# The last attention head of a two-layer diffusion backbone: output products moved into its first two steps, and half a tile ahead in the others

## The chip, the cores and the metric

The kernel runs on one core of one Trainium2 chip. The metric is the device time of one execution in microseconds (us). In the profile PE is the matrix engine (PEld its weight loads), DVE the vector engine, ACT the scalar engine, POOL the GpSimd engine and SP the engine that issues most DMAs.

## The reference

Two layers over 1024 latent tokens of width 1024, with a context of 256 tokens. Layer 0 is a latent attention with 16 heads, layer 1 a differential attention with 8 heads. The change concerns the end of layer 1, where the context gets no output (`need_ctx` is false). Per head of 128 columns, with scale 1/8:

```python
def combine(o1, o2, gate):
    o = o1 - lam_full.astype(o1.dtype) * o2
    o = rms_norm(o, g_sub) * (1.0 - lambda_init)
    return gated(o, gate)                      # o * silu(gate)
q, k, v, gate = project(h, True)
q_c, k_c, v_c, gate_c = project(h_c, False)
o1, o1_c = prefix_attention(q[..0:1], k[..0], v, ...)   # softmax over 1024 + 256 keys
o2, o2_c = prefix_attention(q[..1:2], k[..1], v, ...)
...
x = layer_norm(DEEPNORM_ALPHA * x + gate[:, None, :] * (o @ out_w[i]), ln_g[i], ln_b[i])
```

`o` is 1024 x 1024 (8 heads of 128 columns), `out_w[1]` is 1024 x 1024; the output is `x` after layer 1.

## The kernel before, in words

**Tiles.** The 1024 tokens are 8 tiles `t` of 128. Layer 1 works head by head; a head takes its tiles one after the other, pipelined over three steps: scores of tile t (`scores1`, L1342 and L1343, then maxima on DVE, L1355 to L1361, exponentials on ACT, L1365, sums and the combination of the two softmaxes into one `p` on DVE, L1368 to L1371), turning `p` on PE by transposes (`turn1`, L1378, then `split16`: a half `ph` on ACT, L181, and its rest `pl` on DVE, L182), and the values (`values1`, L1386 to L1388: ten chunks of three matmuls; scaling on ACT, L1391 and L1392, rstd on POOL, L159 and L160). `step1` writes one such step: scores of tile s, values of tile s - 2, turning of tile s - 1, and between them work of a side generator.

**The last head.** In head 7 the side work is the output projection. Its input for a tile is `ws`, 128 x 1024: seven heads come from memory (`out_load`: DMA of the heads' outputs and of the gates, a product on POOL, L1479), column block 7 comes from the head itself (L1397 on DVE). `out_turn` transposes blocks of `ws` on PE (L1491) and splits them into `wx` (ACT, L176) and `wy` (DVE, L177). `mm3` (L185 to L187) is one product: three matmuls of 512 columns, hi x hi, hi x lo, lo x hi, for one block k of 8 and one half `hh` of the output. A tile has 16 products, in two PSUM banks `y[0]`, `y[1]`. `out_tile1(t)` writes them: k = 0 to 6 of half 0, k = 0 to 3 of half 1, then the turn of column block 7, k = 4 to 6 of half 1, then k = 7 of both. Then residual (L1526), layer norm (L1527 to L1543) on DVE, POOL and ACT, and the store; the last tile's layer norm has a form of its own.

**Steps.** Call step s the one with the scores of tile s; steps 8 and 9 have no scores. `out_tile1(s - 2)` runs in steps 2 to 9, `out_turns(s - 1)`, the first seven blocks of the next tile, is woven into it after its 9th and 12th yields. Tile 0's is put ahead in step 2. Steps 0 and 1 have no products. `SLOT1` and `SLOTO` are budgets in units of columns that say how much side work goes between the parts of a step.

**Order.** PE's order is the order in which the program is written (`MAN1`); the other engines' orders and DMA issues come from a scheduler, within the rotating buffers: 8 PSUM banks (tag "b"), and SBUF buffers by tag. Each engine's order is fixed when the kernel is built. The gates of head 7 go through memory like those of the others (`sg_d`); its Silu (L1327) and the split of its values into `vh`, `vl` are written by `prod_v1` in head 6's last steps and run in step 0. `out_open` splits the four late blocks (k = 4 to 7) of the output weight (`oHL`, L1468, L1469 and L176, L177); the first four (`NOW`) are there before.

## Time and profile before

| | |
|---|---|
| median of 3 runs | 1781.78 us (1780.85 to 1781.8) |
| profiled execution | 1781.43 us, span 1779.5 us (1.93 us lie around it) |
| mean granted clock | 0.992 |
| PE, DVE, ACT, POOL busy | 94%, 69%, 63%, 45% of the span |
| step 0, 1, 2 (windows) | 11.4, 9.6, 19.1 us |
| steps 3 to 7 | 17.0 us each |
| steps 8, 9 | 14.8, 13.0 us |
| after PE's last matmul | 8.5 us |

The profile gives busy time of engines in windows, instructions in order of time with the idle time before them and what ended it, and totals of waits. Times of the timeline are in us from the span's start; head 7's first score stands at 1618.34 and PE's last matmul ends at 1771.01.

### The profile page before, as it was taken

Reading aid. Unit: us, or ns where it says so; the run is one execution under the profiler, and the core shown is the slowest. Engines: PE = TensorE matmul, PEld = TensorE weight load, DVE = VectorE, ACT = ScalarE, POOL = GpSimd, SP = SyncE. Lnnn points to the kernel's source line nnn. Section 1 sums busy time; section 2 is a strip of 40 time slices with the busy share of each in tenths; the row PEclk is TensorE's granted clock in tenths of the full one; section 3 lists DMA queues with packets and bytes.
Section 4 is the critical chain, followed back from the end, with each engine's and each line's share of the span. In section 5 each row is a group of like instructions: output and inputs, shape, how many; then the busy total and the mean of one; then the engine's idle time right before and its main releaser. Section 6 shows DMA issues by size and latency. Waiting matters only on the chain. (4 is left out here: it accounts for less than half of the span.)

```text
span 1779.5 us, 36756 instructions
## 1 busy us (share of the span) xinstructions
PE 1664.8 (94%) x14564; PEld 1233.5 (69%) x14564; DVE 1230.8 (69%) x2045; ACT 1119.5 (63%) x2235; POOL 800.3 (45%) x724
## 2 busy tenths in 40 slices
PE   7999999899999998999999999999998999888998
PEld 7999966566666665577866766667675757566876
DVE  7658575665665657557747787787777777868664
ACT  2551177777777787845536676767676766758542
POOL 1532147667776676845541222222313131455454
PEclk9999999999999999999999999999999999999999
DMA  8258520111111113164432212131312122232331
GB/s 301 86 151 261 161 68 22 40 46 27 36 45 34 46 42 85 47 217 166 148 108 76 55 50 74 55 79 55 81 55 60 38 61 61 68 119 67 108 110 71
DMA packets 111225, 154.84 MB, mean 87 GB/s; under 512 B 13415, under 2 KB 84679, under 8 KB 111054
## 3 DMA queue, kind: packets, MB, share of 16 engines
q1 hardware_dynamic: 102654, 144.90, 27.1%
q10 hardware_dynamic: 8400, 7.61, 1.3%
q8 instruction: 114, 1.87, 0.5%
q14 instruction: 57, 0.47, 0.1%
HBM read 98.65 MB, written 27.07 MB: 71 GB/s over the span
## 5 line engine op out<-in xcount | busy, mean ns | idle before, releaser
L779 POOL TENSOR_TENSOR pl<-p,ph 128x1024 f16<-128x1024 f32 (+1 forms) x176 | 364.7, 2078 | 146.4 <-ACT ph L778 120.6
L1365 ACT ACTIVATE p<-ps_b,mx 128x512 f32<-128x512 f32 (+1 forms) x384 | 230.7, 618 | 84.0 <-DVE mx L1361 82.9
L777 ACT ACTIVATE p<-ps_a,esc 128x1024 f32<-128x1024 f32 (+1 forms) x176 | 189.2, 1075 | 93.2 <-PE ps_a L835 87.2
L759 DVE TENSOR_REDUCE mx<-ps_a 128x1 f32<-128x1024 f32 x128 | 155.3, 1222 | 126.9 <-PE ps_a L757 126.8
L778 ACT CAST ph<-p 128x1024 f16<-128x1024 f32 (+1 forms) x176 | 177.1, 1006 | 5.5
L1359 DVE TENSOR_REDUCE mx<-ps_b 128x1 f32<-128x512 f32 x256 | 166.0, 681 | 0.3 <-PE ps_b L1343 0.3
L848 PE MATMUL ps_d<-Vh,pl 128*128 128x65 f16 x1344 | 146.0, 194 | 3.3 <-POOL pl L779 3.3
L845 PE MATMUL ps_d<-Vh,ph 128*128 128x65 f16 x1344 | 148.1, 195 | 0.0
L847 PE MATMUL ps_d<-Vl,ph 128*128 128x64 f16 x1344 | 146.9, 193 | 0.0
L845 PEld LDWEIGHTS <-ph 128*128 128x128 f16 x1344 | 123.2, 97 | 18.0 <-issue 4.6
L1342 PE MATMUL ps_b<-KS,QS 128*128 128x512 f16 (+1 forms) x384 | 127.7, 349 | 7.5 <-DVE pl L182 4.1
L1390 POOL TENSOR_TENSOR sm<-sm,us 128x1 f32<-128x1 f32 x64 | 19.3, 302 | 252.7 <-DVE sm L1369 248.3
L847 PEld LDWEIGHTS <-ph 128*128 128x128 f16 x1344 | 123.9, 98 | 12.1
L1378 PE MATMUL ps_b<-idr,p 128*128 128x128 f32 x640 | 104.1, 278 | 29.9 <-ACT p L1365 15.7
L1343 PE MATMUL ps_b<-KS,Q 128*128 128x512 f16 (+1 forms) x384 | 130.5, 349 | 0.0
L833 PE MATMUL ps_a<-qH,KH 100*128 100x512 f16 x320 | 121.5, 380 | 9.0 <-ACT p L777 4.7
L182 DVE SCALAR_TENSOR_TENSOR pl<-ps_b,lcf,ph 128x512 f16<-128x512 f32 (+1 forms) x192 | 117.2, 654 | 13.7 <-ACT ph L181 13.6
L848 PEld LDWEIGHTS <-pl 128*128 128x128 f16 x1344 | 123.1, 97 | 4.6 <-POOL pl L779 4.6
L181 ACT ACTIVATE ph<-ps_b,lcf 128x512 f16<-128x512 f32 (+1 forms) x192 | 115.4, 649 | 17.3 <-PE ps_b L1378 17.3
L834 PE MATMUL ps_a<-qH,KL 96*128 96x512 f16 x320 | 121.3, 379 | 0.0
L835 PE MATMUL ps_a<-qL,KH 96*128 96x512 f16 x320 | 120.7, 377 | 0.0
L1378 PEld LDWEIGHTS ps_b<-idr,p 128*128 128x128 f32 x640 | 77.6, 143 | 57.1 <-ACT p L1365 24.5
(435 smaller groups left out, 5282.2 us busy)
## 6 DMA issues: line engine op xcount, KB each, us to landing
ws<-in_dw SPq DMA_DIRECT2D x28, 512.0 KB, 4.0
adw<-in_ada_w SPq DMA_DIRECT2D x24, 512.0 KB, 4.6
adaw<-in_ada_w SPq DMA_DIRECT2D x16, 512.0 KB, 7.5
g<-sg_d SPq DMA_DIRECT2D x16, 512.0 KB, 9.0
sg_d<-gg ACTq DMA_DIRECT2D x40, 128.0 KB, 3.5
o_d<-op SPq DMA_DIRECT2D x7, 640.0 KB, 3.9
xt<-in_xT SPq DMA_DIRECT2D x16, 256.0 KB, 4.6
wgs<-in_w_in SPq DMA_DIRECT2D x32, 128.0 KB, 2.3
```

What stands on the lines that cost most here:

```text
L759: dve.tensor_reduce(mx[:, t, 0:1], ps, axis=AX.X, op=ALU.max)
L777: act.activation(p32[:, :n], st, AF.Exp, scale=esc0)
L778: act.copy(ph[:, :n], p32[:, :n])
L779: pool.tensor_tensor(pl[:, :n], p32[:, :n], ph[:, :n], op=ALU.subtract)
L845: pe.matmul(pv[:, t, :], ph[:, ts], Vh[:, k, h, :], start=(k == kcs[0] and t == 0), stop=False, skip_group_check=True)
L847: pe.matmul(pv[:, t, :V0], ph[:, ts], Vl[:, k, h, :], start=False, stop=False, skip_group_check=True)
L848: pe.matmul(pv[:, t, :], pl[:, ts], Vh[:, k, h, :], start=False, stop=(k == NT - 1), skip_group_check=True)
L1342: pe.matmul(out, qs[m][:, ts], ks[m][:, c0:c0 + n], start=True, stop=False)
L1343: pe.matmul(out, q1[m][:, ts], ks[m][:, c0:c0 + n], start=False, stop=True)
L1359: dve.tensor_reduce(mx[:, 2 + 2 * m + i:3 + 2 * m + i], b, axis=AX.X, op=ALU.max, negate=True)
L1365: act.activation(p[m][:, c0:c0 + n], b, AF.Exp, bias=nb, accum_out=sm[:, 2 + 3 * m + i:3 + 3 * m + i])
L1378: pe.transpose(st[:, j * P:(j + 1) * P], pc[:, (k0 + j) * P:(k0 + j + 1) * P], idn)
```

## The change

Products of the output are spread anew over head 7's steps, in a new generator `out_step(s)`, with a tile in work `a = s - 2` and a tile ahead `b = s - 1`:

- step 0: eight products of tile 0 (both halves, k = 0 to 3), with the split of the late weights woven in; step 1: six (k = 4 to 6), with the turn of tile 1;
- step 2: seven products of tile 1, half 0, the column block of tile 0, and closing k = 7 of tile 0: nine;
- steps 3 to 7: half 1 of tile a (k = 0 to 6), with tile b's turn woven in (after 3 and 5 products), then k = 0 to 3 of half 0 of tile b, the turn of column block 7 of tile a, k = 4 to 6 of half 0 of tile b, and the closing products: sixteen;
- step 8: half 1 of tile 6, four products of tile 7, column block, closing: thirteen; step 9: the rest, twelve.

So eleven products stand between the values of a step and the column's turn. Loads of tiles 0 and 1 and tile 0's turn go into head 6's last steps. Head 7's gates stay in the chip's memory (`g7`); their Silu and the value split are written after step 1 (`out_gates`). Source lines move by one to 38 rows: L159 and L160 are now L160 and L161, L176 and L177 are L177 and L178, L182 is L183, L185 to L187 are L186 to L188, L1361 is L1369, L1365 is L1373, L1368 to L1371 are L1376 to L1379, L1397 is L1403, L1491 is L1507, L1542 and L1543 are L1580 and L1581.

```diff
+SLOTF = 0, 4800, 3200, 3200, 3200
...
-        later.append(top)
+        if h < H1 - 1:
+            later.append(top)
+        else:
+            og.update(Vf=Vf, gg=gg, uv=uv)
...
-            oo, g = og[t]
-            c = slice(h * P, (h + 1) * P)
-            dve.scalar_tensor_tensor(oo[:, c], o, ss[:, 1:2], g[:, c], op0=ALU.mult, op1=ALU.mult)
+            dve.scalar_tensor_tensor(og[t][:, DH:], o, ss[:, 1:2], og["g7"][:, t, :], op0=ALU.mult, op1=ALU.mult)
...
+    def out_gates():
+
+        vt[H1 - 1] = vh, vl = w1("vh"), w1("vl")
+        split16(vh, vl, og["Vf"], kc1)
+        prv.close()
+        wg1 = a1.enter_context(spool("a1outg", side="right"))
+        og["g7"] = wg1.tile(GG[0], GG[1], name="g7")
+        flat = lambda x: x.rearrange("p t d -> p (t d)")
+        act.activation(flat(og["g7"]), flat(og["gg"]), AF.Silu, scale=og["uv"])
...
+    def out_step(s):
+
+        a, b = s - 2, s - 1
+        early, late_ = range(NOW), range(NOW, KT - 1)
+        if s == 0:
+            yield from weave(chain(out_mm(0, 0, early), out_mm(0, 1, early)), out_split(), (0, 2, 4, 6))
+            return
+        if s == 1:
+            yield from weave(chain(out_mm(0, 0, late_), out_mm(0, 1, late_)), out_turns(1), (1, 4))
+            return
+        res = w1("res")
+        sp.dma_start(res, zn_d[a * P:(a + 1) * P, :])
+        end = SEQ // P - 1
+        if a == end:
+            yield from out_mm(a, 0, late_)
+        if a:
+            yield from weave(out_mm(a, 1, range(KT - 1)), out_turns(b), (3, 5))
+        if b <= end:
+            yield from out_mm(b, 0, early if a else range(KT - 1))
+        out_turn(a, KT - 1, 1)
+        yield 256
+        if a and b < end:
+            yield from out_mm(b, 0, late_)
+        yield from out_close(a, res)
...
-        for hh in range(2):
-            for k in range(KT - 1):
-                mm(hh, k)
-                yield 1600
-                if hh == 1 and k == 3:
-                    out_turn(t, KT - 1, 1)
-                    yield 256
...
-                    G = weave(out_tile1(t - 2), out_turns(t - 1), (9, 12)) if t >= 2 else iter(())
-                    if t == 2:
-                        G = chain(out_turns(0), G)
+                    G = out_step(t)
                     credit[0] = 0
-                step1((h, t), G, SLOT1 if not last else SLOTO)
+                step1((h, t), G, SLOT1 if not last else SLOTF if t < 2 else SLOTO)
                 if last:
                     for _ in G:
                         pass
+                    if t == 1:
+                        out_gates()
```

PE in step 4, before: the fourth product of the older tile's second half (bank ps_b_22683), the turn of the next tile's `ws_22411` between. All products of this step read `wx_22540` and `wy_22541`, which were turned in step 3:

```order
L1491 MATMUL ps_b_22732<-idr,ws_22411 128x128 x4
L185 MATMUL ps_b_22683<-oH_12515,wx_22540 128x512
L186 MATMUL ps_b_22683<-oL_12516,wx_22540 128x512
L187 MATMUL ps_b_22683<-oH_12515,wy_22541 128x512
L1491 MATMUL ps_b_22742<-idr,ws_22206 128x128
```

PE in step 4, after: the turn of tile 3's `ws_22435`, the last product of tile 2's second half (bank ps_b_22706), and the first product of tile 3 (bank ps_b_22752):

```order
L1507 MATMUL ps_b_22743<-idr,ws_22435 128x128 x3
L186 MATMUL ps_b_22706<-o_3360_22003,wx_22529 128x512
L187 MATMUL ps_b_22706<-o_3361_22004,wx_22529 128x512
L188 MATMUL ps_b_22706<-o_3360_22003,wy_22530 128x512
L186 MATMUL ps_b_22752<-oH_12509,wx_22719 128x512
L187 MATMUL ps_b_22752<-oL_12510,wx_22719 128x512
L188 MATMUL ps_b_22752<-oH_12509,wy_22720 128x512
```

The last three rows read `wx_22719` and `wy_22720`, which come from the turn in the same step.

DVE in step 4, before: the column's gate, the softmax sums and the combination, `pl`, and then `wy_22731` of tile 3:

```order
L1397 SCALAR_TENSOR_TENSOR ws_22206<-o_3472_22671,ss_22673,g_22207 128x128
L1368 TENSOR_REDUCE sm_22607<-sm_22607 128x2
L1369 RECIPROCAL sm_22607<-sm_22607 128x2
L1370 SCALAR_TENSOR_TENSOR sm_22607<-sm_22607,nlam 128x1
L1371 SCALAR_TENSOR_TENSOR p_3464_22608<-p_3465_22609,sm_22607,p_3464_22608 128x1280
L182 SCALAR_TENSOR_TENSOR pl_22700<-ps_b_22701,lcf,ph_22699 128x512
L182 SCALAR_TENSOR_TENSOR pl_22700<-ps_b_22720,lcf,ph_22699 128x512
L177 TENSOR_TENSOR wy_22731<-ps_b_22732,wx_22730 128x512
```

DVE in step 4, after: the same start, then `wy_22720` of tile 3.

```order
L1403 SCALAR_TENSOR_TENSOR ws_22282<-o_3475_22695,ss_22697,g_22280 128x128
L1376 TENSOR_REDUCE sm_22631<-sm_22631 128x2
L1377 RECIPROCAL sm_22631<-sm_22631 128x2
L1378 SCALAR_TENSOR_TENSOR sm_22631<-sm_22631,nlam 128x1
L178 TENSOR_TENSOR wy_22720<-ps_b_22721,wx_22719 128x512
L183 SCALAR_TENSOR_TENSOR pl_22732<-ps_b_22733,lcf,ph_22731 128x512
L178 TENSOR_TENSOR wy_22720<-ps_b_22743,wx_22719 128x384
L1379 SCALAR_TENSOR_TENSOR p_3467_22632<-p_3468_22633,sm_22631,p_3467_22632 128x1280
```

`wy` stands ahead of the combination now, and still behind the column's gate.

POOL in step 9, before: statistics of tile 6's layer norm (mv), the rstd (ss) of tile 7's column, then the two passes over tile 6's z:

```order
L160 TENSOR_TENSOR mv_23499<-mv_23499,neghalf 128x1
L1540 TENSOR_SCALAR mv_23499<-mv_23499 128x1
L159 TENSOR_SCALAR ss_23541<-ss_23541 128x1
L160 TENSOR_TENSOR ss_23541<-ss_23541,neghalf 128x1
L1542 TENSOR_TENSOR z_23487<-z_23487,wsq_21984 128x1024
L1543 TENSOR_TENSOR z_23487<-z_23487,gb_3254_21283 128x1024
```

POOL in step 9, after:

```order
L161 TENSOR_TENSOR mv_23514<-mv_23514,neghalf 128x1
L1578 TENSOR_SCALAR mv_23514<-mv_23514 128x1
L1580 TENSOR_TENSOR z_23497<-z_23497,wsq_22001 128x1024
L160 TENSOR_SCALAR ss_23556<-ss_23556 128x1
L1581 TENSOR_TENSOR z_23497<-z_23497,gb_3254_21283 128x1024
L161 TENSOR_TENSOR ss_23556<-ss_23556,neghalf 128x1
```

The two rows of ss moved behind the first and the second pass.

More of the change, by code (lines that the diff above doesn't have):

```diff
@@ L1202, in hybrid_kernel @@
             "kr": ([P, NTOK], F32, 1), "kH": ([P, NTOK], F16, 1), "kL": ([P, NTOK], F16, 1)}
-    TAGV = {"rr": ([P, 512], F32, 1), "gg": ([P, SEQ // P, P], F32, 1), "Vf": ([P, NT, P], F32, 1)}
+    TAGV = {"rr": ([P, 512], F32, 1), "Vf": ([P, NT, P], F32, 1)}
+    GG = [P, SEQ // P, P], F32, 1
     TAGO = {"res": ([P, D], F32, 2), "z": ([P, D], F32, 2), "gb3": ([P, D], F32, 1),
@@ L1218, in hybrid_kernel @@
     gate1 = wo4.tile([P, D], F32, name="gate1")
+    rot(wo4, GG[0], GG[1], "gg", GG[2], first=True)
+    place["gg"], TAG1["gg"] = wo4, GG
     wv1 = prv.enter_context(spool("a1projv", side="right"))
@@ L1300, in prod_v1 @@
         gg, Vf = w1("gg"), w1("Vf")
-        vt[h] = vh, vl = w1("vh"), w1("vl")
+        vh, vl = w1("vh"), w1("vl")
+        vt[h] = vh, vl
         vT = w1("rr")[:, :CTX]
@@ L1453, in out_open @@
     def out_open():
-        prv.close()
-        wg1 = a1.enter_context(spool("a1outg"))
-        place["g"] = wg1
-        TAG1["g"] = ([P, D], F32, 2)
         og["gb2"] = w1("wsq")
@@ L1462, in out_open, with out_split @@
         oHL.extend([r[:, k - NOW, :] for r in rest] for k in range(NOW, KT))
-        out_load(0)
+    def out_split():
         for k, w in enumerate(pre):
@@ L1469, in out_open, with out_load @@
                 dve.scalar_tensor_tensor(oHL[NOW + k][1], w, gsub, fv(oHL[NOW + k][0]), op0=ALU.mult, op1=ALU.subtract)
-            if k == 0:
-                out_load(1)
-    def out_load(t):
+            yield 0
+    def out_gates():
[6 more added lines that the diff above has]
+        act.activation(flat(og["g7"]), flat(og["gg"]), AF.Silu, scale=og["uv"])
+    def out_load(t, g_tag="gg"):
         ts = slice(t * P, (t + 1) * P)
-        o, g = og[t] = w1("ws"), w1("g")
+        o, g = w1("ws"), w1(g_tag)
+        og[t] = o
         sp.dma_start(o[:, :DH], o_d[1][ts, :DH])
-        sp.dma_start(g, sg_d[1][ts, :])
+        if g_tag == "gg":
+            g = g.rearrange("p t d -> p (t d)")
+        sp.dma_start(g[:, :DH], sg_d[1][ts, :DH])
         pool.tensor_tensor(o[:, :DH], o[:, :DH], g[:, :DH], op=ALU.mult)
@@ L1483, in out_turn @@
     def out_turn(t, k0, n):
-        o, _ = og[t]
+        o = og[t]
         if k0 == 0:
@@ L1501, in out_turns, with out_mm, out_close @@
         yield 768
-    def out_tile1(t):
-        ts = slice(t * P, (t + 1) * P)
-        tH, tL = oT[t]
-        res = w1("res")
-        sp.dma_start(res, zn_d[ts, :])
-        y = [bank("b") for _ in range(2)]
-        def mm(hh, k):
-            c = slice(hh * 512, hh * 512 + 512)
-            mm3(y[hh], tH[:, k, :], tL[:, k, :], oHL[k][0][:, c], oHL[k][1][:, c], k == 0, k == KT - 1)
-        for hh in range(2):
-            for k in range(KT - 1):
-                mm(hh, k)
-                yield 1600
-                if hh == 1 and k == 3:
-                    out_turn(t, KT - 1, 1)
-                    yield 256
+    oy = {}
+    def out_mm(t, hh, ks):
+        tH, tL = oT[t]
+        c = slice(hh * 512, hh * 512 + 512)
+        for k in ks:
+            if k == 0:
+                oy[t, hh] = bank("b")
+            mm3(oy[t, hh], tH[:, k, :], tL[:, k, :], oHL[k][0][:, c], oHL[k][1][:, c], k == 0, k == KT - 1)
+            yield 1600
+    def out_step(s):
[21 more added lines that the diff above has]
+        yield from out_close(a, res)
+    def out_close(t, res):
+        ts = slice(t * P, (t + 1) * P)
         z, bs = w1("z"), w1("bs")
         for hh in range(2):
-            mm(hh, KT - 1)
+            for _ in out_mm(t, hh, (KT - 1,)):
+                pass
             c = slice(hh * 512, hh * 512 + 512)
-            dve.tensor_tensor(z[:, c], y[hh], res[:, c], op=ALU.add)
+            dve.tensor_tensor(z[:, c], oy[t, hh], res[:, c], op=ALU.add)
             dve.bn_stats(bs[:, hh, :], z[:, c])
@@ L1602, in v_last, with out_first @@
             yield from weave(prod_v1(h), chain(*[out_w1(k, lambda: w1("ws")) for k in range(NOW)],
-                                               *[out_pre(k) for k in range(NOW, KT)]), range(1, 36, 2))
+                                               out_first(0), *[out_pre(k) for k in range(NOW, KT)],
+                                               out_first(1)), range(1, 36, 2))
+            yield from out_turns(0)
+        def out_first(t):
+            out_load(t, "wsq")
+            yield
         g1 = gate_row1()
@@ L1613, in hybrid_kernel @@
             else:
-                while later:
-                    later.pop(0)()
                 out_open()
@@ L1631, in hybrid_kernel @@
         for t in range(SEQ // P - 2, SEQ // P):
-            G = weave(out_tile1(t), out_turns(t + 1), (9, 12))
+            G = out_step(t + 2)
             credit[0] = 0
```

## The prediction

> **What bounds the kernel now.** I read the busy shares first, then a table of windows cut at the steps of layer 1's last head, then the timelines of each engine in those windows, and the totals of waits.

> ```profile
> PE 1664.8 (94%) x14564; PEld 1233.5 (69%) x14564; DVE 1230.8 (69%) x2045; ACT 1119.5 (63%) x2235; POOL 800.3 (45%) x724
> ...
> 1618.30:1629.70 11.40, 5.55 (x54) 4.10 (x53) 11.33 (x16) 11.34 (x15) 6.24 (x5) 0.91 0.32 86
> 1629.70:1639.30 9.60, 7.47 (x53) 4.81 (x52) 6.88 (x12) 7.71 (x26) 7.61 (x7) 0.75 0.48 181
> 1639.30:1658.40 19.10, 18.19 (x117) 14.13 (x115) 13.92 (x28) 11.09 (x32) 6.44 (x9) 1.00 0.18 59
> 1658.40:1675.40 17.00, 17.00 (x110) 13.47 (x110) 11.36 (x24) 8.57 (x22) 8.21 (x9) 1.00 0.36 120
> 1675.40:1692.30 16.90, 16.90 (x109) 13.41 (x108) 11.26 (x24) 8.57 (x22) 8.91 (x10) 1.00 0.37 122
> ...
> 1743.20:1758.00 14.80, 14.80 (x97) 12.27 (x96) 6.56 (x13) 5.20 (x10) 7.00 (x8) 1.00 0.21 72
> 1758.00:1771.00 13.00, 13.00 (x80) 10.63 (x79) 3.58 (x8) 2.28 (x5) 6.57 (x7) 1.00 0.10 40
> ```

> The last seven rows are windows: from and to, length, then busy time of PE, weight loads, DVE, ACT, POOL, the granted clock, the DMA share and GB/s. They are steps 0 to 4, 8 and 9. In steps 3 to 9 PE is busy for all of the window: any wait put there is paid in full. Steps 0 and 1 have PE at 5.55 of 11.40 and at 7.47 of 9.60 us, with DVE and ACT full in step 0. The change may win only what PE idles in the first three steps:

> ```profile
> 1629.07 0.69 PE L1378 MATMUL ps_b<-idr,p 128*128 128x128 f32 x2 [5.85 <-DVE pl L182]
> 1630.53 0.63 PE L1342 MATMUL ps_b<-KS,QS 128*128 128x512 f16 x1
> 1638.19 1.29 PE L1378 MATMUL ps_b<-idr,p 128*128 128x128 f32 x10 [2.13 <-DVE p L1371]
> 1639.31 0.27 PE L1342 MATMUL ps_b<-KS,QS 128*128 128x256 f16 x1
> 1675.82 0.38 PE L1342 MATMUL ps_b<-KS,QS 128*128 128x512 f16 x1
> ...
> L185 PE MATMUL ps_b<-oH,wx 128*128 128x512 f32 x8 | 3.4, 428 | 0.6 <-ACT wx L176 0.6
> L187 PE MATMUL ps_b<-oH,wy 128*128 128x512 f32 x8 | 3.2, 406 | 0.3 <-DVE wy L177 0.3
> ```

> The brackets are idle time: 5.85 and 2.13 us; the two grouped rows (lines and shapes of 1618 to 1658) add 0.6 and 0.3. Together 8.9 us. After the gap of 5.85 us the matmuls of 512 columns take 0.63 us where step 4 has 0.38, and the window's clock is 0.75; of a 9.60 us window that is 0.25 x 9.60 = 2.4 us more. After the gap of 2.13 us they run at 0.27 for 256 columns again, no loss. So at most 11.3 us can be won in steps 0 to 2. [...]

> **The change, part by part.** *A, steps 0 to 2.* All 384 matmuls of the products remain; 23 products of three matmuls now lie in steps 0 to 2 where 16 were, so work moves and only PE's idle time counts. What was idle is filled, but DVE and ACT don't get shorter:

> ```profile
> 1620.15 0.68 DVE L1355 TENSOR_REDUCE mx<-ps_b 128x2 f32<-128x512 f32 x1
> 1628.28 1.40 DVE L182 SCALAR_TENSOR_TENSOR pl<-ps_b,lcf,ph 128x512 f16<-128x512 f32 x2
> ...
> L1327 ACT ACT_TABLE_LOAD x1 | 1.3, 1283 | 0.0
> L182 DVE SCALAR_TENSOR_TENSOR vl<-Vf,kc,vh 128x1280 f16<-128x1280 f32 x1 | 1.5, 1544 | 0.0
> ```

> DVE works from 1620.15 to 1629.68 without a gap. The split of the values (1.54 us on DVE) and the Silu with its table load (1.28 us) move from step 0 to behind step 1, where step 2's exponentials need their table back: another 1.28. I put the waits that stay at 5.8 us: about 1.4 for score banks that DVE's maxima and pl must first free, 2.05 in step 2 for p (a combine and a pl after the last exponential, which now stands behind Silu and loads), 1.5 for the values of tile 0, whose split now comes late, and 0.85 small ones. These are estimates from those durations; the bounds are 0 and the 11.3 of before. A = 5.8 - 11.3 = -5.5, from -11.3 to 0. Gate stores and loads of head 7 vanish from the queues; no PE wait of steps 3 to 9 hangs on them, so I give them nothing.

> *B, steps 3 to 7.* Here I see the price. In before, PE needs a tile's turned rows (wx, wy) a whole step after DVE and ACT wrote them. After the change the half tile ahead (four products of tile b, first half) reads wx and wy written in the same step. Where they come, in step 4 (start 1675.38):

> ```profile
> 1675.38 0.28 PE L1342 MATMUL ps_b<-KS,QS 128*128 128x256 f16 x1
> 1677.96 0.20 DVE L1530 BATCH_NORM_AGGREGATE mv<-bs 128x2 f32<-128x12 f32 x1
> 1679.48 1.25 ACT L1541 ACTIVATE z<-z,mv 128x1024 f32<-128x1024 f32 x1 [5.51 <-POOL mv L1540]
> 1680.81 2.39 POOL L1542 TENSOR_TENSOR z<-z,wsq 128x1024 f32<-128x1024 f32 x1 [1.36 <-ACT z L1541]
> 1683.56 2.40 POOL L1543 TENSOR_TENSOR z<-z,gb 128x1024 f32<-128x1024 f32 x1
> 1685.92 0.54 POOL L160 TENSOR_TENSOR ss<-ss,neghalf 128x1 f32<-128x1 f32 x1
> 1686.50 0.35 DVE L1397 SCALAR_TENSOR_TENSOR ws<-o,ss,g 128x128 f32<-128x128 f32 x1 [5.50 <-POOL ss L160]
> 1687.15 0.22 DVE L1370 SCALAR_TENSOR_TENSOR sm<-sm,nlam 128x1 f32<-128x1 f32 x1
> ...
> DVE ws L1397 <- POOL ss L160: 27.5, 5, 5.5
> L177 DVE TENSOR_TENSOR wy<-ps_b,wx 128x512 fp32r<-128x512 f32 x8 | 5.5, 685 | 1.2 <-ACT wx L176 1.2
> L176 ACT CAST wx<-ps_b 128x512 fp32r<-128x512 f32 x8 | 4.7, 585 | 3.8 <-PE ps_b L1491 3.8
> L1365 ACT ACTIVATE p<-ps_b,mx 128x512 f32<-128x512 f32 x12 | 8.2, 688 | 2.9 <-DVE mx L1361 2.0 <-DVE p L1371 0.8
> ```

> The layer norm of the tile closed before goes DVE, POOL, ACT, then two POOL passes of 2.4 us; the rstd (ss) of the head's column stands behind the second one, and DVE's column gate L1397 waits for it, 5.5 us in each of five steps. DVE serves its queue in order, so every row after it waits as well. In after this order is kept (now L1403 behind POOL's L1580, L1581 and L161), and the wy of the tile that PE wants stands behind it and the three short softmax rows L1376 to L1378. Counted from the step's start: L1397 at +11.12, L1370 ends at +11.99, wy takes 0.685: ready at +12.7. When does PE ask?

> ```profile
> 1679.20 0.48 PE L185 MATMUL ps_b<-oH,wx 128*128 128x512 f32 x1
> 1759.67 0.48 PE L185 MATMUL ps_b<-oH,wx 128*128 128x512 f32 x1
> 1767.29 0.27 PE L1491 MATMUL ps_b<-idr,ws 128*128 128x128 f32 x1
> 1687.07 0.60 PE L1491 MATMUL ps_b<-idr,ws 128*128 128x128 f32 x4
> 1687.42 0.48 PE L185 MATMUL ps_b<-oH,wx 128*128 128x512 f32 x1
> ```

> Scores and values fill 1679.20 - 1675.38 = 3.82 us. A product matmul has a pitch of (1767.29 - 1759.67) / 33 = 0.231 us; 7 products of the older tile are 4.85. Four turns cost 1687.42 - 1687.07 = 0.35, and three such groups stand among them: 1.05. So the first product of the tile ahead is due at about +9.7, its third matmul, the first that reads wy, at about +10.3 with a start-up. PE waits 12.7 - 10.3 = 2.4 us. It works in order: values, scores and closing products behind that matmul all wait, and through them the next layer norm, so the next step's chain starts later by as much and the wait recurs. Steps 4 to 7: 4 x 2.4 = 9.6. In step 3 one of the two bias rows of the exponentials (L1369) stands behind L1403 too, so four exponentials come before the cast of wx. From +11.47 (L1397's end): about 0.3 for the bias, two exponentials of 0.688 and two of half the columns that I put at 0.5, a cast of 0.585, wy 0.685: +15.4, a wait of 5.1. B = 9.6 + 5.1 = +14.7. If each end is off by half a microsecond, five waits give 2.5 to either side. What would spare it is PE being late for another reason, or wy ahead of L1403; neither is so.

> *C, steps 8 and 9.* Eleven products from the values to the column's turn mean that behind the last turn nothing covers the cast and the subtraction.

> ```profile
> 1762.56 0.35 DVE L1397 SCALAR_TENSOR_TENSOR ws<-o,ss,g 128x128 f32<-128x128 f32 x1 [2.23 <-POOL ss L160]
> 1762.98 2.42 POOL L1542 TENSOR_TENSOR z<-z,wsq 128x1024 f32<-128x1024 f32 x1 [0.45 <-ACT z L1541]
> 1767.60 0.27 ACT L176 CAST wx<-ps_b 128x128 fp32r<-128x128 f32 x1 [4.70 <-PE ps_b L1491]
> 1767.90 0.29 DVE L177 TENSOR_TENSOR wy<-ps_b,wx 128x128 fp32r<-128x128 f32 x1 [4.98 <-ACT wx L176]
> ```

> Before, three products hid 0.27 + 0.29; now 0.55 in step 8 is bare and in step 9 0.83 (with the turn). In step 9 POOL's order is also turned: ss was ahead of both passes, now it stands behind both. 1762.98 is +4.96 after step 9's start (1758.02); two passes, ss and the gate put the column at 4.96 + 2.42 + 2.40 + 0.54 + 0.35 = +10.7, while PE has 1.65 of values and ten products (6.93), +8.6. The last pl of the values stands behind the z adds and bn_stats of step 8, which I put at 1.1 of PE's time. So +9.7 against +10.7: 1.0 more. C = 0.55 + 0.83 + 1.0 + 1.1 = +3.5, from 1.4 to 4.6.

> **The sum.** -5.5 + 14.7 + 3.5 = +12.7 us. The profiled run took 1781.43 (1.93 around the span), 0.35 under the median of 1781.78: 1781.43 + 12.7 = 1794.1 us. A measurement here tells some 0.2%, 3.6 us, from no change.

> **Rivals.** *The wait for wy does not bind*, the other side: if wx and wy were ready by +10.3, B is nil, and A + C = -2.0: 1779.4. It decides at 2.4 us of the chain, and the chain would have to be about a quarter shorter; for it speaks that POOL's two passes may run quicker beside less other work, against it that five waits of five reached about 5.5. If A also came near its end, 1776 would be faster. Chance 0.13. *The clock falls in step 3*: its wait of 5.1 us is nearest to the 5.85 gap, which cost 2.4; 1796.5. For: that gap; against: the gap of 2.13 cost nothing, and two matmuls on wx break this one a little ahead of its end. Chance 0.22. [...] *The first steps do not contract*: waits stay at 11.3, as DVE's and ACT's full rows would have it; 1799.6, chance 0.09. *They run without waits*: 1788.3, chance 0.06. My own case has 0.50.

> **How the numbers follow.** 1794.1 is the likeliest case. The low end takes the first steps without waits and the five waits at half a microsecond less: 1788.3 - 2.5 = 1785.8, set at 1785.5; the high end, the first steps not contracted: 1799.6. Outside lie the wy rival and combinations of the others. Faster by over 0.2% is only the better half of that rival, 0.06; within 0.2% its rest and a little of the low end, 0.08; slower 0.86.

> **What would show it.** Windows of steps 4 to 7 of about 19.3 us instead of 17.0, with PE idle about 2.3 before L188, put down to DVE wy L178, and DVE's L1403 waiting for POOL ss L161. A longer wait, near 5, in step 3. In steps 0 to 2 no PE gap over 3 us and a clock of 1.00, step 3 starting near 1658. In step 9 PE waiting for the column's turn. I am wrong if steps 4 to 7 stay near 17 us, if DVE wy comes before +10.3, or if the first steps still hold a gap of 5 us.

## Result and the profile after

The changed kernel takes 1800.84 us (median of 4 runs, 1798.21 to 1803.37) against 1781.79 for the kernel before (4 runs): a ratio of 1.0103, with a 95% interval of 1.0088 to 1.0118. That is 19.05 us slower. The forecast was 1794.1 with a range of 1785.5 to 1799.6: the direction is right, the time lies 1.2 us above the range. The profiled run took 1800.92 us, its span is 1799.1 us.

The windows of the changed kernel, cut at its steps 0 to 9 (from and to, length, busy time of PE, weight loads, DVE, ACT and POOL, granted clock, DMA share, GB/s):

```profile
1619.75:1630.30 10.55, 10.55 (x79) 8.19 (x76) 10.55 (x16) 9.83 (x20) 5.61 (x4) 1.00 0.33 94
1630.30:1643.13 12.83, 10.31 (x78) 7.88 (x78) 8.07 (x17) 11.07 (x29) 5.77 (x8) 1.00 0.25 72
1643.13:1660.64 17.51, 14.04 (x82) 10.44 (x80) 11.97 (x24) 7.00 (x22) 1.40 (x5) 0.90 0.12 43
1660.64:1683.37 22.73, 18.71 (x110) 14.41 (x108) 11.99 (x25) 9.49 (x24) 8.70 (x10) 0.92 0.25 88
1683.37:1702.68 19.31, 17.54 (x109) 13.29 (x109) 11.52 (x24) 8.34 (x22) 8.72 (x10) 1.00 0.30 103
1702.68:1723.55 20.87, 19.09 (x109) 14.51 (x109) 11.59 (x24) 8.34 (x22) 8.81 (x10) 0.92 0.28 95
1723.55:1742.84 19.29, 17.52 (x109) 13.29 (x108) 11.50 (x24) 8.34 (x22) 8.78 (x10) 1.00 0.30 103
1742.84:1763.70 20.86, 19.11 (x109) 14.49 (x108) 11.59 (x24) 8.34 (x22) 8.57 (x9) 0.92 0.15 51
1763.70:1777.07 13.37, 13.02 (x88) 10.75 (x88) 6.40 (x13) 4.72 (x9) 6.52 (x7) 1.00 0.23 80
1777.07:1790.60 13.53, 10.87 (x69) 8.37 (x66) 3.68 (x8) 2.64 (x6) 6.49 (x7) 1.00 0.10 39
```

Step 0 has no idle PE any more. Steps 4 and 6 last 19.3 us, as forecast, where 17.0 stood before. Steps 5 and 7 have the same instructions, about the same idle time (20.87 - 19.09 = 1.78), and last 1.6 us longer: their granted clock is 0.92. Steps 2 and 3 have the low clock too (0.90 and 0.92). The PE timeline of the changed kernel, with the idle time in brackets (steps 1 to 5 and 9):

```profile
1634.20 0.38 PE L1350 MATMUL ps_b<-KS,QS 128*128 128x512 f16 x1 [2.00 <-DVE pl L183]
...
1645.94 0.38 PE L1350 MATMUL ps_b<-KS,QS 128*128 128x512 f16 x1 [1.78 <-DVE pl L183]
...
1674.74 0.79 PE L186 MATMUL ps_b<-oH,wx 128*128 128x512 f32 x1 [4.02 <-ACT wx L177]
...
1696.01 0.50 PE L188 MATMUL ps_b<-oH,wy 128*128 128x512 f32 x1 [1.76 <-DVE wy L178]
1696.35 0.40 PE L186 MATMUL ps_b<-oH,wx 128*128 128x512 f32 x1
...
1715.32 0.60 PE L188 MATMUL ps_b<-oH,wy 128*128 128x512 f32 x1 [1.75 <-DVE wy L178]
1715.72 0.63 PE L186 MATMUL ps_b<-oH,wx 128*128 128x512 f32 x1
...
1788.27 0.30 PE L1507 MATMUL ps_b<-idr,ws 128*128 128x128 f32 x1 [1.59 <-DVE ws L1403]
```

The waits stand where the forecast put them: the first matmul that reads wy of the tile ahead (L188) in steps 4 and 5, the one that reads wx in step 3, the column's turn in step 9. Behind the wait of 1.76 us in step 4 a matmul takes 0.40 us, behind the wait of 1.75 in step 5 it takes 0.63. The chain to wy in step 4, from DVE's timeline and then POOL's:

```profile
1694.48 0.35 DVE L1403 SCALAR_TENSOR_TENSOR ws<-o,ss,g 128x128 f32<-128x128 f32 x1 [5.48 <-POOL ss L161]
...
1695.27 0.68 DVE L178 TENSOR_TENSOR wy<-ps_b,wx 128x512 fp32r<-128x512 f32 x1
```

```profile
1688.80 2.40 POOL L1580 TENSOR_TENSOR z<-z,wsq 128x1024 f32<-128x1024 f32 x1 [1.36 <-ACT z L1579]
...
1691.56 2.38 POOL L1581 TENSOR_TENSOR z<-z,gb 128x1024 f32<-128x1024 f32 x1
1693.90 0.55 POOL L161 TENSOR_TENSOR ss<-ss,neghalf 128x1 f32<-128x1 f32 x1
```

The gate L1403 starts 11.11 us after the step (1683.37), wy lands at 12.6: the forecast had 11.12 and 12.7.

### The profile page after: what moved, and what is told of

The parts are those of the page before. It is cut to its first block, busy times and chain, and to the rows that moved or that the text cites. A ratio compares the mean times of both kernels' runs of the same rounds, so it can differ in the third digit from the quotient of the medians.

```text
span 1799.1 us, 36754 instructions
## 1 busy us (share of the span) xinstructions
PE 1671.8 (93%) x14564; PEld 1236.1 (69%) x14564; DVE 1230.0 (68%) x2045; ACT 1116.7 (62%) x2235; POOL 794.9 (44%) x724
## 3 DMA queue, kind: packets, MB, share of 16 engines
q10 hardware_dynamic: 8400, 7.61, 1.3%
## 5 line engine op out<-in xcount | busy, mean ns | idle before, releaser
L1373 ACT ACTIVATE p<-ps_b,mx 128x512 f32<-128x512 f32 (+1 forms) x384 | 230.5, 617 | 87.4 <-DVE mx L1369 87.1
L182 ACT ACTIVATE ph<-ps_b,lcf 128x512 f16<-128x512 f32 (+1 forms) x192 | 115.2, 649 | 36.6 <-PE ps_b L1386 36.6
L183 DVE SCALAR_TENSOR_TENSOR pl<-ps_b,lcf,ph 128x512 f16<-128x512 f32 (+1 forms) x192 | 117.8, 654 | 21.1 <-ACT ph L182 21.1
```

Source lines behind the costliest of these rows:

```text
L1373: act.activation(p[m][:, c0:c0 + n], b, AF.Exp, bias=nb, accum_out=sm[:, 2 + 3 * m + i:3 + 3 * m + i])
```

## Experiments

The theory: the rows queued on DVE behind its wait for POOL's rstd are late for the half tile ahead; PE idles for them in steps 3 to 7; and behind idle PE the clock can fall, which costs again (1.6 us in each of steps 5 and 7). The rivals: reading rows in the step of their turn is late by itself; the slow stretches (matmuls at the low clock) are not from idleness; the loss lies in the first steps.

**The column's gate cut in two.**

```diff
-            dve.scalar_tensor_tensor(og[t][:, DH:], o, ss[:, 1:2], og["g7"][:, t, :], op0=ALU.mult, op1=ALU.mult)
+            dve.tensor_tensor(og[t][:, DH:], o, og["g7"][:, t, :], op=ALU.mult)
+            pool.tensor_scalar(og[t][:, DH:], og[t][:, DH:], ss[:, 1:2], None, op0=ALU.mult)
```

> The changed kernel, with the column's gate cut in two: DVE multiplies by the gate alone (no wait for POOL), and POOL multiplies by rstd right behind its rstd. DVE's order stays row for row what it was. Theory (the rows queued behind DVE's wait for POOL's rstd cost the stall in steps 3 to 7, and the stall costs clock): wy is ready near +11.1 instead of +12.6, steps 3 to 7 fall from 22.7, 19.3, 20.9, 19.3, 20.9 to some 17.2 to 17.6 us each, no window of them under a clock of 0.98, and the kernel takes about 1785 us (1783 to 1788). Rival (reading rows in the step in which they are turned is late by itself, because ACT's cast stands behind six exponentials): wy still near +12.5, steps of 19 us or more, 1797 us or more.

Measured: 1791.15 us, where about 1785 was expected, beside 1782.85 for the kernel before, ratio 1.0048 (1.0028 to 1.0067). Windows of steps 3 and 4, PE's timeline in step 4, and DVE's and POOL's there:

```profile
1657.35:1675.50 18.15, 17.47 (x111) 13.28 (x108) 13.36 (x25) 9.49 (x24) 9.41 (x10) 1.00 0.34 110
1675.50:1694.12 18.62, 17.54 (x110) 13.30 (x109) 13.44 (x24) 8.45 (x22) 9.44 (x11) 1.00 0.34 106
```

```profile
1686.60 0.50 PE L186 MATMUL ps_b<-oH,wx 128*128 128x512 f32 x1 [0.96 <-ACT wx L177]
```

```profile
1681.14 2.35 DVE L1403 TENSOR_TENSOR ws<-o,g 128x128 f32<-128x128 f32 x1 [0.33 <-ACT o L1399]
1683.41 0.26 DVE L1369 TENSOR_SCALAR mx<-mx 128x1 f32<-128x1 f32 x1
```

```profile
1680.94 2.40 POOL L1581 TENSOR_TENSOR z<-z,wsq 128x1024 f32<-128x1024 f32 x1 [1.36 <-ACT z L1580]
```

The wait for wy is all but gone (0.12 us before L188 in step 4), the low clock in steps 3 to 7 with it, and step 3 falls from 22.73 to 18.15. Steps 3 to 7 together fall from 103.06 to 92.41 us, beside 84.8 in the kernel before. But each of steps 4 to 7 still takes 18.5 to 18.6, where 17.2 to 17.6 was expected: PE now waits 0.96 us for ACT's cast of wx, which stands behind the exponentials. Part of that is this edit's own price: the bare gate on DVE takes 2.35 us, as long as the POOL pass that began 0.2 us before it, and holds back a bias of the exponentials (L1369), for which ACT waits 0.83 us. So DVE's wait for POOL is shown as the larger part of the loss over steps 3 to 7, low clock included; how much of the rest a gate without this price would leave, this run doesn't show.

**The wait filled with work.**

```diff
-            if k == 0:
+            if k == 0 and (t, hh) not in oy:
...
+        if a and b < end:
+            oy[b, 0] = bank("b")
+            for i in range(17 if a == 1 else 7):
+                pe.matmul(oy[b, 0], oT[a][0][:, i % 4, :], oHL[i % 4][0][:, :512], start=True, stop=True)
```

> The changed kernel, with extra matmuls of no use (overwritten in the same bank by the product that follows) in front of the half tile ahead: 17 in step 3, 7 in each of steps 4 to 7. They fill the wait of PE with work of 0.23 us each. Theory (after an idle wait the clock is granted at half for some 3.4 us, depending on when the wait falls): DVE's wy comes when it came before, so the time of the wait is the same, but steps 3, 5 and 7 lose their slow stretch: steps of 19.3 to 19.6 us throughout, step 3 near 21, a clock of 1.00 in all, about 1796 us. Rival (the slow stretches in steps 5 and 7 have nothing to do with idleness): steps 5 and 7 stay at 20.9 or grow by the filling, 1801 us or more.

Measured: 1798.49 us (1.0083, 1.0063 to 1.0102). Windows of steps 3 to 6:

```profile
1662.63:1685.66 23.03, 21.09 (x127) 16.55 (x125) 12.00 (x25) 9.49 (x24) 8.84 (x10) 1.00 0.25 86
1685.66:1704.97 19.31, 18.84 (x116) 14.68 (x115) 11.49 (x24) 8.36 (x22) 8.74 (x9) 1.00 0.29 103
1704.97:1724.33 19.36, 18.89 (x117) 14.70 (x116) 11.52 (x24) 8.35 (x22) 8.91 (x10) 1.00 0.30 102
1724.33:1743.63 19.30, 18.83 (x116) 14.67 (x115) 11.49 (x24) 8.35 (x22) 8.65 (x9) 1.00 0.31 104
```

With seven more matmuls in each step, step 5 is 1.5 us shorter than without them (19.36 against 20.87), and the clock is 1.00 in all of steps 3 to 7: the slow stretches are the price of idleness. Step 3 gained nothing, since the 17 matmuls ended 1.9 us after the rows had come. A second kernel with 8 there:

> As the filled wait, but with 8 extra matmuls in step 3, which end before the rows come (17 ended 1.9 us after). Theory (idleness sets the clock): step 3 falls from 22.7 to about 21.0 us, steps 4 to 7 at 19.3, clock 1.00 in all of them. Rival: step 3 stays at 22.7.

Steps 4 to 7 were 19.30 to 19.33 us again; its one run took 1797.98. Step 3 missed the expectation, at 22.56. Its windows row and its PE row:

```profile
1659.90:1682.46 22.56, 20.59 (x118) 15.97 (x115) 11.99 (x25) 9.50 (x24) 8.90 (x10) 0.92 0.28 88
```

```profile
1671.95 2.34 PE L1551 MATMUL ps_b<-oH,wx 128*128 128x512 f32 x6 [1.97 <-ACT p L1373]
```

The filling itself waited 1.97 us for its bank, and the step's clock is 0.92.

**The first steps alone.** Steps 3 to 9 are put back to sixteen products of one tile, with no half tile ahead and the column's turn after eleven of them; step 2 keeps only the two closing products. The new lines stand in place of the half tile ahead and the column's turn behind it:

```diff
...
+        if a == 0:
+            out_turn(a, KT - 1, 1)
+            yield 256
+        else:
+            def main():
+                yield from out_mm(a, 0, range(KT - 1))
+                yield from out_mm(a, 1, early)
+                out_turn(a, KT - 1, 1)
+                yield 256
+                yield from out_mm(a, 1, late_)
+            yield from weave(main(), out_turns(b), (9, 12))
```

> The changed kernel without the half tile ahead: tile 0's fourteen products in steps 0 and 1 and the gates on chip as changed, step 2 with two closing products only, and steps 3 to 9 as in the kernel before (16 products of one tile each, the column's turn after eleven products with three behind it). Theory (the loss lies in the half tile ahead, the first steps are about neutral or a gain): steps 3 to 7 at 17.0 us, 8 at 14.8, 9 at 13.0; step 2 falls to 12 to 14 us where DVE bounds it; about 1779 us (1776 to 1783). Rival (the first steps lose what is lost, by tables and waits): over 1790 us.

Measured: 1782.93 us, ratio 1.0000 (0.9990 to 1.0009). Windows of steps 2, 3 and 4:

```profile
1644.24:1659.27 15.03, 10.50 (x62) 7.88 (x60) 10.13 (x21) 6.80 (x21) 2.05 (x4) 0.77 0.15 48
1659.27:1678.15 18.88, 17.10 (x110) 13.43 (x108) 13.47 (x29) 10.04 (x25) 8.15 (x11) 1.00 0.34 105
1678.15:1695.11 16.96, 16.96 (x109) 13.44 (x109) 11.32 (x24) 8.56 (x22) 8.91 (x10) 1.00 0.35 117
```

The half tile ahead, with the ends that go with it, holds the loss: without it step 4 is at 16.96 again. But the first steps gain nothing by themselves (3.9 us over the expected 1779): the idle time moves into steps 2 and 3 (4.5 and 1.8 us), and step 2 has the low clock, 0.77.

**Turned two steps ahead.** Step s turns tile s, into a third pair of buffers:

```diff
-            oT[t] = [w1(tg).bitcast(F32R).rearrange("p (a b) -> p a b", a=KT) for tg in ("wx", "wy")]
+            third = "3" if t % 3 == 2 else ""
+            oT[t] = [w1(tg + third).bitcast(F32R).rearrange("p (a b) -> p a b", a=KT) for tg in ("wx", "wy")]
...
-            yield from weave(out_mm(a, 1, range(KT - 1)), out_turns(b), (3, 5))
+            yield from weave(out_mm(a, 1, range(KT - 1)), out_turns(s), (3, 5))
...
```

> The changed kernel with tiles turned one step earlier: step s turns tile s instead of tile s - 1, into a third pair of buffers for wx and wy; the half tile ahead then reads rows turned in the step before. Head 7's gates lie where the gate row lay, to make room. DVE still waits for POOL's rstd as in the changed kernel. Theory (only reading in the same step is dear): no wait of PE for wx or wy in steps 3 to 7, 17.0 to 17.5 us each, clock 1.00, head 7 in about 163 us against 161.2 before and 179.4 changed, near 1784 us in all. Rival (half a tile ahead costs by itself, through banks or DVE's order): steps of 19 us.

Measured: 1786.75 us, 1.0021 (1.0011 to 1.0030). Windows of steps 3 and 4:

```profile
1662.12:1681.47 19.35, 17.38 (x110) 13.28 (x108) 11.73 (x25) 9.38 (x24) 9.07 (x10) 1.00 0.32 103
1681.47:1698.60 17.13, 17.13 (x109) 13.37 (x109) 11.32 (x24) 8.34 (x22) 8.67 (x10) 1.00 0.34 116
```

DVE's order is the changed one, its gate still waits 5.50 us for POOL in step 4, and PE waits for nothing there: half a tile ahead is all but free (17.13 beside 16.96) when its rows come a step earlier. Step 3 has a wait left (1.97 us, for a bank that the exponentials still read).

**The cast on DVE.** The gate cut in two, and wx of the first four blocks of tiles 2 to 7 on DVE:

```diff
-    split(f(tH), f(tL), tb[:, :n * P])
+    split(f(tH), f(tL), tb[:, :n * P], e_hi=dve.tensor_copy if t > 1 and n == 4 else None)
```

> The kernel with the split column gate, and in addition the cast of the first four turned blocks (wx) on DVE instead of ACT, for tiles 2 to 7: DVE's order then has cast and wy ahead of the softmax sums, behind nothing that waits for POOL or for the exponentials. Theory (the 0.96 us that PE still waited per step with the gate split come from ACT's cast, which stands behind the exponentials): PE's wait in steps 4 to 7 falls under 0.3 us, steps of 17.4 to 17.7 us instead of 18.6; the time from head 7's first score to the end falls from 168.7 to about 164 us. Rival (DVE's own work is the bound): steps stay at 18.5 us or grow.

Measured: 1783.15 us, 1.0002 (0.9993 to 1.0011). Steps 3 and 4:

```profile
1657.17:1674.12 16.95, 16.95 (x110) 13.44 (x108) 13.96 (x26) 9.01 (x23) 10.85 (x11) 1.00 0.38 117
1674.12:1691.41 17.29, 17.27 (x109) 13.37 (x108) 14.04 (x25) 7.97 (x21) 9.77 (x11) 1.00 0.34 115
```

PE is busy but for 0.02 us. Turning in the same step costs 0.3 us a step (17.29 beside 16.96) instead of 2.3 and more when cast and subtraction stand behind neither POOL nor the exponentials; the clock is 1.00 in each of steps 0 to 4.

**The ends.** In step 8 two of the four early products behind the turn:

```diff
-            yield from out_mm(b, 0, early if a else range(KT - 1))
+            yield from out_mm(b, 0, range(2) if b == end else early if a else range(KT - 1))
         out_turn(a, KT - 1, 1)
         yield 256
-        if a and b < end:
-            yield from out_mm(b, 0, late_)
+        if a and b <= end:
+            yield from out_mm(b, 0, range(2, 4) if b == end else late_)
```

> The changed kernel, but in step 8 two of tile 7's four early products stand behind the column's turn instead of ahead of it. Step 9 is untouched. Theory: the 0.35 us of PE's wait for the cast behind the turn in step 8 goes, steps 3 to 7 as in the changed kernel, so 1800 us, not to be told from it. Rival (an uncovered turn costs much): step 8 falls by over 1 us.

Measured: 1799.50 us (1.0096, 1.0081 to 1.0111); step 8 fell from 13.37 to 12.82, by 0.55. The low clock came in steps 3, 5 and 6 here (0.93, 0.92 and 0.92) and not in 4 or 7 (1.00), where the changed kernel had it in 3, 5 and 7: the steps that lose it change from kernel to kernel, with the same instructions in them.

Then this, tiles turned two ahead, and the end of step 9 and tile 6's layer norm:

```diff
         if a == end:
             yield from out_mm(a, 0, late_)
+            yield from out_mm(a, 1, early)
+            out_turn(a, KT - 1, 1)
+            yield 256
+            yield from out_mm(a, 1, late_)
+            yield from out_close(a, res)
+            return
...
-        if t == SEQ // P - 1:
+        if t >= SEQ // P - 2:
```

> Turned two ahead, and the ends mended: in step 8 two products stand behind the column's turn, in step 9 three, and tile 6's layer norm takes the last tile's form on DVE, so that POOL's rstd of the last column stands behind no pass. Theory: step 8 at 12.8 us, step 9 at about 11.3 instead of 13.5, head 7 in about 160.5 us, 1781 us in all, no slower than before. Rival: the wait only moves to DVE, where tile 6's four passes of 0.7 us stand ahead of the column's gate, and step 9 stays over 12.5.

Measured: 1781.25 us, 0.9997 (0.9987 to 1.0007). Steps 8 and 9:

```profile
1745.61:1757.59 11.98, 11.98 (x82) 10.04 (x82) 5.05 (x11) 3.55 (x7) 6.52 (x7) 1.00 0.27 89
1757.59:1768.70 11.11, 10.41 (x69) 8.37 (x66) 6.49 (x12) 1.51 (x5) 3.38 (x4) 1.00 0.13 47
```

Step 9 is 2.4 us shorter than in the changed kernel; the wait for POOL's rstd behind two passes is gone.

**A control on the kernel before**:

```diff
-            dve.scalar_tensor_tensor(oo[:, c], o, ss[:, 1:2], g[:, c], op0=ALU.mult, op1=ALU.mult)
+            dve.tensor_tensor(oo[:, c], o, g[:, c], op=ALU.mult)
+            pool.tensor_scalar(oo[:, c], oo[:, c], ss[:, 1:2], None, op0=ALU.mult)
```

> The kernel before, with the column's gate split between DVE and POOL and nothing else. Theory (before the change DVE's wait for POOL's rstd lay beside PE's work, since the rows it delayed were read a step later): steps 3 to 7 stay at 17.0 us, the time the same within 0.2%, 1780 to 1784 us. Rival (that wait costs in any case): 2 us or more less.

Measured: 1781.94 us, 1.0001 (0.9991 to 1.0010), steps 3 to 7 at 16.96, with PE busy for all of them as without the edit. Taking the gate out of DVE's wait gains nothing in the kernel before. The control is not a full one: DVE then waits 2.50 us at the softmax sums (L1368), which start only 0.8 us sooner in the step.

**All that helped together**: on the changed kernel the diffs of the gate cut in two, of the cast on DVE, of step 8 and of the ends, without turning two ahead.

> The changed kernel with everything that helped put together: the column's gate split between DVE and POOL, wx cast on DVE, in step 8 two products and in step 9 three behind the column's turn, tile 6's layer norm on DVE. Theory: steps 3 to 7 at 17.0 to 17.3 us as with the cast on DVE, step 8 at 12.0 to 12.8, step 9 at 11.1, no PE wait over 1 us after step 2; from head 7's first score to the end about 157 us (161.2 before, 179.4 changed), some 1778 us, 0.2% under the kernel before. Rival: the parts get in each other's way on DVE, and it stays at 1781 or more.

Measured: 1777.98 us against 1781.85 for the kernel before (11 and 21 runs), ratio 0.9981 (0.9972 to 0.9990). Steps 4, 8 and 9:

```profile
1674.12:1691.41 17.29, 17.27 (x109) 13.37 (x109) 14.05 (x25) 7.97 (x21) 9.64 (x11) 1.00 0.34 115
1743.18:1755.99 12.81, 12.81 (x89) 10.72 (x89) 6.85 (x14) 4.02 (x8) 7.16 (x8) 1.00 0.25 83
1755.99:1767.13 11.14, 10.44 (x69) 8.37 (x66) 6.33 (x13) 1.51 (x5) 4.00 (x5) 1.00 0.13 47
```

It beats both kernels, the one before by about 3.9 us. Its profile says where: steps 0 to 2 take 39.03 - 40.07 - 4.85 = -5.9 us against the kernel before, steps 3 to 7 take 86.02 - 84.8 = +1.2, steps 8 and 9 take 23.95 - 27.80 + 4.85 = +1.0 (4.85 is the seven products that moved). So the first steps' filling pays once the half tile ahead and the ends cost little.

## Why the prediction was right and wrong

| term, us | forecast | measured in the profiles |
|---|---|---|
| A, steps 0 to 2 | -5.5 | 40.89 - 40.07 - 4.85 (seven more products) = -4.0 |
| B, steps 3 to 7 | +14.7 | 103.06 - 84.8 = +18.3 |
| C, steps 8 and 9 | +3.5 | 26.90 - 27.80 + 4.85 = +4.0 |
| start of head 7 | 0 | +1.4 |
| sum | +12.7 | +19.6 (1799.1 - 1779.5, by rounding) |

*Place and mechanism* were right. The gate L1403 came at +11.11, wy at +12.6, the waits are on L188 <- DVE wy L178, and steps 4 and 6 are 19.3. The gate cut in two takes these waits and the low clock of steps 3 to 7 away; rows turned a step earlier, or cast and subtracted ahead of the wait, bring step 4 to 17.1 and 17.3. That DVE's wait was free before is seen in PE, busy for all of steps 3 to 7 there with it and, in the control, without it.

*The step that failed is the clock.* The prediction priced it once, at 2.4 us in step 3 with a chance of 0.22. It put it at nothing in step 2, where it expected a clock of 1.00, and at nothing in steps 4 to 7: the only gap of that size that it had, 2.13 us before, had cost nothing. That was one case taken for a rule. Waits of 1.75 us cost 1.6 us in steps 5 and 7 and nothing in 4 and 6. By the granted clock, step 2 lost 0.10 x 17.51 = 1.75, step 3 0.08 x 22.73 = 1.8, steps 5 and 7 1.6 each: 6.75 us together, and the sum lacks 6.9. Without them A would be -5.8 and B 13.3. What else was off (A by -0.3, B by -1.4, C by +0.5, the start of head 7 by +1.4) cancels to 0.2, and that is luck.

How much idleness takes the clock can't be read from one gap that did and one that did not, 5.85 and 2.13 us: here 1.75 us was enough twice.

*Smaller points.* The wait in step 3 was 4.02, not 5.1: wx came at +14.1 (1674.74 - 1660.64), where the sum had 14.7, and wy cost no second wait. In steps 4 to 7 it was 1.76, not 2.4, yet the step grew by 2.35 as forecast. The PE rows around the wait in step 4 start 0.40, 0.34, 2.16 and 0.34 us apart (at 1693.11, 1693.51, 1693.85, 1696.01 and 1696.35), where rows without a wait start 0.23 apart: 2.32 us more in all. Of that 1.93 is the wait for wy, the rest a short wait for wx, which the sum did not have, and two slow starts. PE asked for wy later than the sum had it (about +10.7 against +10.3), so that 2.35 meets 2.4 is in part luck. C's wait of 1.59 in step 9 stood for the forecast 1.0, and the last pl cost 0.7 rather than 1.1. The start of head 7 lay between 1616.8 and 1621.9 in these profiles, also in kernels with the same instructions ahead of it (1618.34 before, 1621.94 in the control), so its 1.4 us is not put down to the change. In A the waits that stay were 5.99 against 5.8, but their parts were others: waits for score banks behind DVE's pl took 2.00 and 1.78 us where the sum had 1.4, p took 0.52 where it had 2.05, the values of tile 0 took 0.51 (a bank that ACT's scaling, L1399, still read) where it had 1.5, and the column's wx and wy took 1.1. That the total fits is luck.

## What to carry to other kernels

Work pulled forward must be checked against the queue of the engine that makes its input: a wait that is free while its product is read a step later becomes the bound when the product is read in the same step (here DVE's wait of 5.5 us, with steps of 17.0 us before and 19.3 and more after). Price an idle gap of the matrix engine with its clock as well, at each place where it recurs, and give its chance from more than one gap: of the eight waits of 1.75 us in two kernels here, four cost 1.6 us more. When filling idle steps gains nothing, look where the idle time went, and mend the queue that holds it first: only all of it together paid here.

## What the hardware showed beyond that

```profile
1691.69:1695.10 3.41, 2.55 (x12) 1.46 (x11) 0.59 (x3) 2.73 (x9) 2.76 (x2) 1.00 0.09 37
1695.10:1698.51 3.41, 2.50 (x13) 2.10 (x14) 3.38 (x6) 0.69 (x1) 0.19 (x1) 1.00 0.31 121
1712.17:1715.58 3.41, 1.64 (x6) 0.75 (x5) 1.73 (x6) 1.56 (x5) 1.77 (x3) 1.00 0.38 154
1715.58:1718.99 3.41, 3.41 (x11) 2.72 (x11) 2.45 (x4) 0.69 (x1) 0.00 (x0) 0.50 0.00 0
1732.65:1736.06 3.41, 1.77 (x9) 0.85 (x6) 1.33 (x6) 1.95 (x6) 2.16 (x3) 1.00 0.32 132
1736.06:1739.47 3.41, 3.28 (x17) 2.71 (x18) 3.32 (x5) 0.81 (x2) 0.00 (x0) 1.00 0.06 22
1753.13:1756.54 3.41, 1.66 (x7) 1.00 (x8) 2.53 (x8) 0.76 (x2) 0.96 (x3) 1.00 0.38 154
1756.54:1759.95 3.41, 3.41 (x13) 2.72 (x11) 2.21 (x2) 0.69 (x1) 0.00 (x0) 0.50 0.00 0
```

In steps 5 and 7 the wait lies whole in one interval of the grid, PE is busy for 1.64 and 1.66 us of it, and the next interval has a clock of 0.50. In steps 4 and 6 a border of the grid cuts the wait, the intervals have PE busy for 1.77 us or more, and the clock stays. Steps 2 and 3 of this trace are sorted in the same way: PE is busy for 1.57 us of the interval from 1643.90 and for none of the one from 1671.21, and the next intervals have 0.50. It doesn't sort all: in the kernel before, PE was busy for 1.55 us of the interval from 1634.51, and the next one had 1.00. What else counts is open.

An estimate from these figures: a wait of 1.75 us that falls anywhere on the grid lies whole in an interval with a chance of (3.41 - 1.75) / 3.41 = 0.49; behind four of the eight the clock fell. With 1.6 us for each, four such waits and 1.8 us for the wait of 4.02 us, as measured, would have put the forecast at about 1799 us.

A DVE multiplication of 128 x 128 (the gate cut in two, L1403, step 4) took 2.35 us while a POOL pass of 2.40 us ran. In step 2 of the same kernel, where POOL was busy for 1.75 of 17.20 us and ran no such pass, the same row took 0.29:

```profile
1648.38 0.29 DVE L1403 TENSOR_TENSOR ws<-o,g 128x128 f32<-128x128 f32 x1 [0.78 <-ACT o L1399]
```

The two rows of step 4 end together, DVE's at 1683.49 and POOL's at 1683.34. No run shows why.
